# A hybrid attention trunk on one core: what follows a product moves one step ahead, two weight casts go ahead of two copies, and the last keys are loaded one phase earlier

## The chip, the core and the metric

The kernel runs on one core of one Trainium2 chip. The metric is the device time of one execution in microseconds (us), lower is better. TensorE (PE) multiplies, VectorE (DVE), ScalarE (ACT) and GpSimd (POOL) work elementwise, SyncE (SP) issues most of the transfers. Each engine works through its own queue in order; engines wait for each other through semaphores.

## The reference

One layer of a decoder trunk on x (2048 x 1024), all in float32. Cut to what matters here:

```python
mod = silu(c) @ w_ada + b_ada
shift, scale, gate = split(mod, 3)
u = x * (1 + scale) + shift
q, k, v, a_gate, p_in, p_gate, m_a, m_p = split(u @ w_in)
a = (sliding_window_sink_attention(q, k, v, sinks, bias, mask) * silu(a_gate)) @ w_attn_proj
p = (grouped(multiscale_causal_pool(p_in)) * pool_scale * silu(p_gate)) @ w_pool_proj
y = (sigmoid(m_a) * a + sigmoid(m_p) * p) @ w_out * (1 + gate)
x = layer_norm(alpha * x + y)
```

The attention has 16 query heads on 2 key heads of width 64. Each block of 128 queries looks at its own block of keys and the one before it, under a causal window of 128, with a relative bias for each head and one sink logit for each head. The pool is a causal mean over 2, 4, 8 or 16 steps, by channel group, less the input.

## The kernel before

**Products.** Every large product runs as a Strassen-like scheme on 2 x 2 blocks, with seven products in place of eight, named B11, T1, T2, B21, T3, B22, T4. A `Quad` holds two tiles of 128 output channels and the raw weights for them (`w`, four blocks of 128 x 512 named by `block`, and `a22`); `sum1`, `mid` and `late` make the sums of the weight blocks. To keep float32 accuracy each operand is split into a high part, rounded to the matmul's type by a cast, and a low part, the rest (`low`, line 131). One `product` (line 317) is therefore 12 matmuls of 128 x 128 by 128 x 512: four contraction tiles, and for each of them high x high, high x low and low x high. A quad has three accumulators in PSUM: a, b and c. B11 and B21 add into a, T1 and B22 into b, T2, T3 and T4 into c. Between the products there is elementwise work: c starts as a copy of a after B11 (`seed`), p5 is a copy of b after T1, b = c + p5 after T2, p5 = c + p5 after T3, and a result is handed on after B21 (a), B22 (b) and T4 (c and p5).

**Phases.** The sequence is cut into two halves of 1024 (s = 0 and 1). For each half there is a ring phase (`ring`, `back`, `front`), which does nothing but products (the gates, the keys and values, the first queries), and then an attention phase (`attention`, line 774). After both halves comes the phase of the projections and the output. `kv_quad` (line 543) is the quad of the keys and values in the ring. When its first result arrives, `place_kv` (line 1521) lays out the tiles `kk` (keys, a high and a low part) and `vv` (values), whose room had been lent to the ring as spare space until then; `take_k` (line 734) fills the keys, `turn_v` (line 720) transposes and fills the values some steps later. Column block 0 of `kk` and `vv` is the last block of the half before. `load_kv` (line 748) fetches it with two transfers from DRAM and does nothing for s = 0.

**The attention phase.** It runs 64 iterations, one for a pair of heads j and a block b of 128 queries (n = 8j + 4t + b), and three more for the end of the pipeline. In iteration n the code emits, in this order: the scores of n on TensorE (`score_mms`: rows `lg<-kk,qs`), the transposes of the probabilities of n-2 (`turn_mms`: rows `pt<-ident,L`), the reciprocal of the sums of n-1, the output of n-3 (`o`), the scaling of n-1, the high part `pth` of n-2, bias and exponential of n (`L`), the low part `ptl` of n-2, then the fill, then the product with the values of n-2 (`value_mms`: rows `pv<-pth,vv` and `pv<-ptl,vv`), and last the work whose time has come (`run_coming`). Every instruction there is emitted through `Ordered` (line 51), so each engine runs them in the order in which they are emitted. Line 57 stands in the profile for all of them.

**The fill.** `filling` (line 947) is a generator that goes through the 93 products of 13 quads (pool mix, merge gates, queries) and two opened ones. It gives out a product in four parts of three matmuls, and each iteration asks for five or six parts, so that 372 parts are spread over 67 iterations (line 1065). `begun(i)` runs before a product, among other things to split the weights of the product three places on (`split`, line 892: cast on ScalarE, low part on POOL or VectorE). `ended(i)` (line 927) emits what follows a product:

```python
if name == "T1":
    p5 = st[x][3] = tp.tile([P, CH], F32, tag="p5", bufs=2, name="p5")
    act.copy(p5, b)
elif name == "T2":
    dve.tensor_tensor(b, c, p5, ALU.add)
elif name == "T3":
    dve.tensor_tensor(p5, c, p5, ALU.add)
```

and for B21, B22 and T4 it calls `take`, which hands the result to the pool (`take_p`: three copies on ScalarE, sums on POOL), to the queries (`take_q`: two instructions on ScalarE and two on VectorE) or to a gate's store (`take_gate`: a copy and a transfer). Because `ended(i)` stands behind the `yield` of the last part, it runs when the next part is asked for, which is in the next iteration if the product ended with an iteration's last part.

**The start of the phase** (lines 985 to 996) emits, ahead of the loop: `load_kv`, the first bias tile, a one-element Exp that loads ScalarE's table (`warm`), the copy of a (`seed(0)`, row `mm<-mm`), the copy of b to p5 (row `p<-mm`), and then the splits of the first three products (T2, B21, T3 of quad 0; rows `w_set<-W`).

Of the kernel before, what the change touches and what calls it, by code (L numbers as in the profile page):

```python
# [60 lines left out]
def kernel(  # L61
# [66 lines left out]
    def as32(ap):  # L128
        return ap.bitcast(F32)

    def low(engine, dst, src, hi):
        engine.tensor_tensor(dst, src, as32(hi), ALU.subtract)  # L132

    def mm(*args, **kw):
        pe.matmul(*args, **kw)
# [6 lines left out]
    def bank(tag="mm"):  # L142
        return ps.tile([P, CH], F32, tag=tag, bufs={"mm": 4, "lg": 2, "pt": 1, "pv": 1}[tag], name=tag)
# [173 lines left out]
    def product(acc, w, name, first=False, i0=0, i1=4):  # L317
        t = sets[name]
        hi, lo = w
        for n, (part, u) in enumerate(((hi, 0), (hi, 1), (lo, 0))):  # L320
            for i in range(i0, i1):
                mm(
                    acc,
                    part[:, i * P : (i + 1) * P],
                    t[:, i, u, :],
                    start=first and i == 0 and n == 0,
                    stop=i == 3 and n == 2,
                    skip_group_check=True,
                )
# [213 lines left out]
    def kv_quad(s):  # L543
        vts = []

        def consume(ph, mi, t, src):
            if mi == 0:
                if t == 0:
                    place_kv(ph)
                take_k(ph, s, t, src)  # L550
            else:
                vt = ph.c("vt")
                nc.scalar.copy(vt, src)
                vts.append((t, vt))

        def turn(ph, i):
            turn_v(ph, s, *vts[i])

        return Quad((win[TK], win[TV]), consume), turn
# [160 lines left out]
    def turn_v(ph, s, t, vt):  # L720
        vtp = bank(("pt", "pv")[t]).rearrange("p (b a d) -> p b a d", b=NB, a=2)
        for b in range(NB):
            pe.transpose(vtp[:, b].rearrange("p a d -> p (a d)"), vt[:, b * P : (b + 1) * P], ident)
        blocks = slice(1 + NB * t, 1 + NB * (t + 1))
        for kv in range(2):
            dst = ph.c("v1", F32R).rearrange("p (b d) -> p b d", b=NB) if kv else vv[:, blocks]
            nc.scalar.copy(dst[:, :, 0:HD], vtp[:, :, kv, :])
            low(nc.vector, dst[:, :, HD:], vtp[:, :, kv, :], dst[:, :, 0:HD])
            if kv:
                sp.dma_start(v_d[s, :, blocks], as32(dst))  # L730
            elif s == 0 and t == 1:
                sp.dma_start(v_end_d, as32(dst[:, NB - 1]))

    def take_k(ph, s, t, kp):
        c0 = P + t * CH
        for kv in range(2):
            rows = slice(kv * HD, kv * HD + HD)
            dst = ph.t.tile([P, 2, CH], F32R, tag="k1", bufs=1, name="k1") if kv else kk[:, :, c0 : c0 + CH]
            for half in (kv, 1 - kv):
                to = slice(half * HD, half * HD + HD)  # L740
                nc.scalar.copy(dst[to, 0, :], kp[rows, :])
                low(nc.vector, dst[to, 1, :], kp[rows, :], dst[rows, 0, :])
            if kv:
                sp.dma_start(k_d[s, :, :, c0 : c0 + CH], as32(dst))
            elif s == 0 and t == 1:
                sp.dma_start(k_end_d, as32(dst[:, :, CH - P :]))

    def load_kv(s):
        if s:
            sp.dma_start(as32(kk[:, :, 0:P]), k_end_d)  # L750
            sp.dma_start(as32(vv[:, 0]), v_end_d)
# [22 lines left out]
    def attention(ph, s, fills, post, opened):  # L774
# [10 lines left out]
        def bias_tile(j):  # L785
            bt = tp.tile([P, 2, 2 * P], F32, tag="bt", bufs=2, name="bt")
            e_src = e_rep[:, 2 * j : 2 * j + 2, :]
            sp.dma_start(bt, bass.AP(e_src.tensor, e_src.offset + P - 1, [[HEADS * ET - 1, P], [ET, 2], [1, 2 * P]]))
            return bt
# [75 lines left out]
        def take(x, mi, t, src, kept=False):  # L865
            kind, m, _ = fills[x]
            if kind == "mix":
                take_p(m + mi, t, src)
            elif kind == "q":
                n = 8 * (m - 2 + mi) + NB * t + NB - 1  # L870
                if kept and n > now_n[0]:
                    later(n, lambda: take_q(m + mi, t, src, act, dve))
                else:
                    take_q(m + mi, t, src, act, dve)
            else:
                take_gate(kind, m + mi, t, src, kept)
# [5 lines left out]
        splits = {}  # L882
# [9 lines left out]
        def split(i):  # L892
            x, name = seq[i]
            q = quads[x]
            if name == "B11" and x > 1:
                q.sum1(pool)
            w = ph.split()
            hi, lo = made[i] = w[:, 0:CH], w[:, CH:]
            act.copy(hi, q.block(name))
            low(dve if name == "T1" or (x, name) in on_dve else pool, lo, q.block(name), hi)  # L900
            if name == "T1":
                q.mid(pool)
            elif name == "B21":
                q.late(pool)

        def begun(i):
            x, name = seq[i]
            if name == "T1":
                st[x][1] = bank()
                if x < K:  # L910
                    later(free_b[0], lambda: seed(x))
                    if free_b[0] < now_n[0]:
                        run_coming()
            if name == "B11":
                st[x] = [bank(), None, None, None]
                if x < K:
                    quads[x + 1].load(ph, False, sp, None)
            if (x, name) == (K - 1, "B22"):
                quads[K + 1].load(ph, False, sp, None)
            for j in splits.get(i, ()):  # L920
                split(j)

        def seed(x):
            st[x][2] = bank()
            act.copy(st[x][2], st[x][0])

        def ended(i):
            x, name = seq[i]
            if x >= K or name == "B11":
                return  # L930
            a, b, c, p5 = st[x]
# [7 lines that stand above are left out]
            elif name == "B21":  # L939
                take(x, 0, 0, a)  # L940
            elif name == "B22":
                take(x, 0, 1, b)
            else:
                take(x, 1, 0, c)
                take(x, 1, 1, p5, True)

        def filling():
            for i, (x, name) in enumerate(seq):
                begun(i)
                w = made.pop(i)  # L950
                acc = st[x][{"B11": 0, "B21": 0, "T1": 1, "B22": 1}.get(name, 2)]
                for k in range(4):
                    product(acc, w, name, name in ("B11", "T1"), k, k + 1)
                    yield
                ended(i)

        def score_mms(j, b, q, x):
            k0 = P if s == 0 and b == 0 else 0
# [25 lines left out]

        N = KT * 2 * NB
        U = 2 * NB
        load_kv(s)
        bts = {0: bias_tile(0)}
        act.activation(warm, mhalf, AF.Exp)
        seed(0)  # L990
        p5 = st[0][3] = tp.tile([P, CH], F32, tag="p5", bufs=2, name="p5")
        act.copy(p5, st[0][1])
        for i in range(-3, 0):
            for j in splits.get(i, ()):
                split(j)
        fill = filling()
        lgs, exps, Ls, pvs, outs, ags = {}, {}, {}, {}, {}, {}
        total, done = 4 * len(seq), 0

        for n in range(N + 3):  # L1000
            now_n[0] = n
            j, t, b = n // U, n // NB % 2, n % NB
# [511 lines left out]
    def rooms_of(name, dt=F32):  # L1514

        q = [kvp.tile([P, D], dt, tag=f"qs{i // 2}{i % 2}", name=f"{name}_qs{i}") for i in range(4)]
        k = kvp.tile([P, 2 * (P + 2 * CH)], F32, tag="kk", name=f"{name}_kk")
        v = kvp.tile([P, (2 * NB + 1) * P], F32, tag="vv", name=f"{name}_vv")
        return q, k, v

    def place_kv(ph):

        nonlocal kk, vv
        ph.turns.clear()
        kk = kvp.tile([P, 2, P + 2 * CH], F32R, tag="kk", name="kk")
        vv = kvp.tile([P, 2 * NB + 1, P], F32R, tag="vv", name="vv")
# [15 lines left out]
    with Pools("g0", spare=2, p=2, c=5) as ph:  # L1542
        started = head(ph, plans[0])
        kq, k, v = rooms_of("first", F32R)
# [7 lines left out]
    with Pools("g1", spare=4, p=2, c=5) as ph:  # L1552
        kq, k, v = rooms_of("second")
# [7 lines left out]
    with Pools("mix", spare=4, p=2, c=8) as ph:  # L1561
# [10 lines left out]
        for n, (raw, i) in enumerate((raw, i) for raw in (ain_d[1], pin_d[1], wo_d) for i in range(4)):  # L1572
            for offset, f in sums_to(ph, raw, i, load_raw(raw, i)):
                at = int(2 + 8 * n + offset)
                i, gi = every[at // 14]
# [78 lines left out]
```

## Time and profile before

| what | us |
|---|---|
| median of 3 runs | 1692.15 |
| lowest and highest run | 1687.09, 1692.64 |
| the profiled execution | 1693.3 |
| its span, first to last instruction | 1691.5 |
| first ring phase ends, first attention phase begins | about 256 |
| second ring phase ends, second attention phase begins | about 830 |
| projections begin | about 1183 |

The profile is of one execution. A span is the time from the first to the last instruction; the execution's own time is 1.8 us longer. Times in rows are us from the span's start. In a row of the timeline the last bracket is the engine's idle time just before, and what ended it. A matmul's duration runs from its start to a modelled end, and matmuls overlap.

### The profile page before, as it was taken

The numbers are of one execution on the slowest core, as the hardware profiler recorded it, in microseconds if no ns is written. First come the engines' busy times: TensorE is split into PE (matmuls) and PEld (weight loads), VectorE is DVE, ScalarE is ACT, GpSimd is POOL, SyncE is SP. The second block draws the span as 40 slices with busy tenths as digits, with TensorE's granted clock in tenths as the row PEclk, the third lists the DMA queues.
The fourth block names the chain that finished last, engine by engine and source line by source line (L and its number), as shares of the span: only waits on it lengthen the run. The fifth ranks groups of instructions, "written<-read, shape, count | busy, mean of one in ns | idle before, by whom it ended". The sixth has DMA issues, their size and how long they took to land.

```text
span 1691.5 us, 24675 instructions
## 1 busy us (share of the span) xinstructions
PE 1648.7 (97%) x8058; PEld 1384.4 (82%) x8058; DVE 1193.7 (71%) x2132; ACT 1030.0 (61%) x2150; POOL 988.5 (58%) x734
## 2 busy tenths in 40 slices
PE   7999999999999999999999999999999999999997
PEld 6788888888888888888788888888878777887886
DVE  6856545676857657357567677676669897989877
ACT  4755457878778755335578777876646445644452
POOL 3343437586857828762476867496567576533442
PEclk9999999999999999999999999999999999999999
DMA  9688843343432478766533344234979797888443
GB/s 359 219 279 307 197 161 102 101 132 108 149 107 99 135 248 308 267 231 211 190 114 99 114 130 156 81 114 135 336 247 363 262 360 259 318 283 271 150 150 112
DMA packets 188849, 336.79 MB, mean 199 GB/s; under 512 B 18336, under 2 KB 44080, under 8 KB 188720
## 3 DMA queue, kind: packets, MB, share of 16 engines
q1 hardware_dynamic: 185600, 330.96, 57.3%
q10 hardware_dynamic: 3088, 4.23, 1.0%
q8 instruction: 64, 1.05, 0.2%
q14 instruction: 65, 0.53, 0.1%
q0 software_dynamic: 32, 0.02, 0.0%
HBM read 227.96 MB, written 110.33 MB: 200 GB/s over the span
## 4 chain that ended last, share of the span: by engine, by line
PE 74%; DVE 8%; DMA 7%; ACT 4%; issue 3%; POOL 3%; SPq 1%; POOLq 0%; DVEq 0%; ACTq 0%
PE mm L57 48%; PE lg L57 19%; PE pv L57 4%; PE pt L57 4%; DVE w_set L132 1%; DMA ain_T<-spare 1%; ACT L L57 1%; DMA g<-ma_d 1%; DMA g<-mp_d 1%; DVE w_set L57 1%; DVE set_T L57 1%; POOL W L269 1%; DMA spare<-pin_B 1%; DVE L L57 1%; ACT w_set L57 1%
## 5 line engine op out<-in xcount | busy, mean ns | idle before, releaser
L57 PE MATMUL mm<-set_B,w_set 128*128 128x512 f32 x2664 | 655.8, 393 | 2.2 <-DVE w_set L132 1.2
L57 PEld LDWEIGHTS mm<-set_B,w_set 128*128 128x128 f32 x2664 | 497.1, 189 | 107.0 <-DVE w_set L132 2.4
L57 PE MATMUL mm<-set_T,w_set 128*128 128x512 f32 x1824 | 455.5, 396 | 5.9 <-DVE mm L57 3.9
L57 PE MATMUL lg<-set_T,w_set 128*128 128x512 f32 x1704 | 412.6, 392 | 10.5 <-DVE p L390 4.4
L57 PEld LDWEIGHTS mm<-set_T,w_set 128*128 128x128 f32 x1824 | 336.7, 189 | 76.2 <-DVE mm L57 6.5
L57 PEld LDWEIGHTS lg<-set_T,w_set 128*128 128x128 f32 x1704 | 319.9, 189 | 81.8 <-ACT w_set L306 5.2
L132 DVE TENSOR_TENSOR w_set<-W,w_set 128x1024 fp32r<-128x1024 f32 x137 | 197.8, 1445 | 142.3 <-ACT w_set L306 129.3
L306 ACT CAST w_set<-W 128x1024 fp32r<-128x1024 f32 x137 | 143.8, 1050 | 212.7 <-PE mm L57 124.3
L57 POOL TENSOR_TENSOR w_set<-W,w_set 128x512 fp32r<-128x512 f32 x120 | 157.3, 1318 | 116.9 <-ACT w_set L57 112.0
L269 POOL TENSOR_TENSOR W<-W,A 128x512 f32<-128x512 f32 x46 | 74.1, 1610 | 232.5 <-DMA A<-in_win_dram 63.5
L57 DVE TENSOR_TENSOR o<-pv,o 64x128 f32<-64x128 f32 x256 | 72.1, 282 | 133.7 <-ACT o L57 127.3
L57 POOL TENSOR_TENSOR spare<-spare 128x512 f32<-128x512 f32 x68 | 124.0, 1826 | 31.5 <-DMA spare<-pin_B 12.2
L57 POOL TENSOR_TENSOR W<-W 128x512 f32<-128x512 f32 x82 | 108.3, 1336 | 53.2 <-DVE sm L57 31.0
L57 ACT ACTIVATE L<-L,nm 128x257 f32<-128x257 f32 (+1 forms) x256 | 127.2, 499 | 9.3 <-DVE nm L57 3.7
L278 POOL TENSOR_TENSOR W<-W 128x512 f32<-128x512 f32 x46 | 72.8, 1583 | 95.9 <-DVE w_set L132 83.5
L57 DVE CUSTOM_DVE_ANT_0 L<-lg,bt,nsink 128x256 f32<-128x256 f32 (+1 forms) x256 | 111.7, 473 | 21.3 <-PE lg L57 11.9
L57 ACT CAST w_set<-W 128x512 fp32r<-128x512 f32 (+1 forms) x165 | 101.4, 628 | 20.9 <-POOL W L57 14.9
L273 POOL TENSOR_TENSOR W<-W 128x512 f32<-128x512 f32 x44 | 72.7, 1656 | 66.3 <-DVE w_set L132 57.2
L57 ACT COPY o<-pv 64x256 f32<-64x256 f32 x128 | 47.4, 370 | 75.9 <-PE pv L57 74.7
L57 DVE TENSOR_TENSOR ptl<-pt,pth 128x512 fp32r<-128x512 f32 (+1 forms) x128 | 85.7, 669 | 1.3 <-ACT pth L57 1.0
L274 POOL TENSOR_TENSOR W<-W 128x512 f32<-128x512 f32 x44 | 71.6, 1628 | 21.9 <-DMA W<-in_win_dram 18.9
L57 ACT ACTIVATE L<-L,sm 128x256 f32<-128x256 f32 (+1 forms) x128 | 64.3, 502 | 31.7 <-DVE sm L57 31.4
(230 smaller groups left out, 2398.2 us busy)
## 6 DMA issues: line engine op xcount, KB each, us to landing
W<-in_win_dram SPq DMA_DIRECT2D x42, 512.0 KB, 5.4
W<-in_win_dram SPq DMA_DIRECT2D x42, 256.0 KB, 3.7
A<-in_win_dram SPq DMA_DIRECT2D x42, 256.0 KB, 4.9
ag_d<-sig SPq DMA_DIRECT2D x32, 256.0 KB, 5.7
pg_d<-sig SPq DMA_DIRECT2D x32, 256.0 KB, 4.4
pg<-pg_d SPq DMA_DIRECT2D x32, 256.0 KB, 3.2
pin_B<-fin SPq DMA_DIRECT2D x32, 256.0 KB, 2.0
ag<-ag_d SPq DMA_DIRECT2D x32, 256.0 KB, 2.9
```

What stands on the lines that cost most here:

```text
L57: return lambda *args, **kw: self.tc.keep_in_program_order(op(*args, **kw))
L132: engine.tensor_tensor(dst, src, as32(hi), ALU.subtract)
L269: e.tensor_tensor(self.w[:, 1, :], self.w[:, 2, :], self.a22, ALU.add)
L273: e.tensor_tensor(x[:, 1, :], x[:, 1, :], x[:, 0, :], ALU.subtract)
L274: e.tensor_tensor(x[:, 2, :], x[:, 0, :], x[:, 2, :], ALU.subtract)
L278: e.tensor_tensor(x[:, 3, :], x[:, 3, :], x[:, 1, :], ALU.subtract)
L306: a.copy(by_two(hi), raw)
```

## The change

Three edits. `load_kv(s)` moves from the start of the attention phase to the moment in the ring where `place_kv` has just laid out the tiles. `ended(i)` is called behind the last part's matmuls and ahead of their `yield`, in place of behind it. At the start of the attention phase the splits of the first two products and `seed(0)` come first, then the one-element Exp, then the copy to p5, then the split of the third product.

```diff
@@ kv_quad
             if mi == 0:
                 if t == 0:
                     place_kv(ph)
+                    load_kv(s)
                 take_k(ph, s, t, src)
@@ filling
                 for k in range(4):
                     product(acc, w, name, name in ("B11", "T1"), k, k + 1)
+                    if k == 3:
+                        ended(i)
                     yield
-                ended(i)
@@ attention
-        load_kv(s)
         bts = {0: bias_tile(0)}
+        for i in (-3, -2):
+            for j in splits.get(i, ()):
+                split(j)
+        seed(0)
         act.activation(warm, mhalf, AF.Exp)
-        seed(0)
         p5 = st[0][3] = tp.tile([P, CH], F32, tag="p5", bufs=2, name="p5")
         act.copy(p5, st[0][1])
-        for i in range(-3, 0):
-            for j in splits.get(i, ()):
-                split(j)
+        for j in splits.get(-1, ()):
+            split(j)
```

## The prediction, made before the changed kernel ran

> **What bounds the kernel now.** First the page: the busy times and the chain that ended last.
>
> ```profile
> PE 1648.7 (97%) x8058; PEld 1384.4 (82%) x8058; DVE 1193.7 (71%) x2132; ACT 1030.0 (61%) x2150; POOL 988.5 (58%) x734
> ...
> PE 74%; DVE 8%; DMA 7%; ACT 4%; issue 3%; POOL 3%; SPq 1%; POOLq 0%; DVEq 0%; ACTq 0%
> ```
>
> TensorE sets the time. The change takes no matmul away, so it can only shorten the moments in which TensorE stands still. It touches the two attention phases and one load in the ring ahead of the second, so I cut the windows view at the two phases:
>
> ```profile
> 256.00:620.00 364.00, 358.71 (x1919) 307.16 (x1918) 245.63 (x675) 272.14 (x735) 254.19 (x207) 1.00 0.38 124
> ...
> 830.00:1183.00 353.00, 349.30 (x1899) 300.58 (x1900) 243.17 (x667) 267.89 (x725) 252.32 (x199) 1.00 0.37 118
> ```
>
> The first numbers are start and length, then the busy times of PE, PEld, DVE, ACT and POOL. TensorE lacks 5.3 us of the first phase and 3.7 us of the second, so the prize is a few us. The longest row of TensorE's waits in the first phase's window and that in the second's (us, times, longest) show one place:
>
> ```profile
> PE mm L57 <- DVE mm L57: 2.4, 2, 1.6
> ...
> PE mm L57 <- DVE mm L57: 1.5, 2, 1.0
> ```
>
> For a yardstick, an iteration of the attention loop without waits, from the chain in order of time (start, us):
>
> ```profile
> 1150.91 0.47 PE pv L57 x4
> 1151.39 0.47 PE lg L57 x4
> 1151.85 0.44 PE pt L57 x4
> 1152.29 4.12 PE mm L57 x18
> ```
>
> 18 product matmuls take 4.12, so 0.23 each. The page's rows give one a duration of 0.39, because they overlap: a wait costs 0.16 more than the idle time shown.
>
> **Part 1: casts ahead of copies.** The start of the first phase, from the timeline (start, us, engine, what, idle before in brackets):
>
> ```profile
> 249.77 1.48 POOL L273 TENSOR_TENSOR W<-W 128x512 f32<-128x512 f32 x1
> 253.69 0.57 ACT L57 COPY mm<-mm 128x512 f32<-128x512 f32 x1 [2.00 <-PE mm L57]
> 256.16 0.56 PE L57 MATMUL lg<-kk,qs 128*128 128x128 f32 x4
> 256.36 0.59 ACT L57 COPY p<-mm 128x512 f32<-128x512 f32 x1 [2.10 <-PE mm L57]
> 256.84 1.66 ACT L57 CAST w_set<-W 128x512 fp32r<-128x512 f32 x3
> 257.51 0.73 PE L57 MATMUL mm<-set_T,w_set 128*128 128x512 f32 x2 [0.80 <-ACT w_set L57]
> 257.54 2.52 POOL L57 TENSOR_TENSOR w_set<-W,w_set 128x512 fp32r<-128x512 f32 x2 [6.29 <-ACT w_set L57]
> 258.87 3.97 PE L57 MATMUL mm<-set_T,w_set 128*128 128x512 f32 x10 [0.62 <-POOL w_set L57]
> 264.26 0.64 PE L57 MATMUL lg<-kk,qs 128*128 128x256 f32 x4
> ```
>
> ScalarE is in order. The cast of the first fill product (T2) stands behind the copy `p<-mm`, which waits for the T1 product to end at 256.16. Yet T2's raw weights are there at 251.25, when POOL's L273 ends. TensorE then waits for the high part, and again for POOL's low part. Iteration 0 should take 0.47 + 4.12 = 4.59 (it has no `pt` and no `pv`). It takes 264.26 - 256.16 = 8.10, so 3.51 too long.
>
> After the change two casts (1.66/3 = 0.55 each) run on ScalarE after 251.25, in the idle time ahead of 253.69. POOL makes two lows (2.52) from about 251.9 to 254.4; its row shows it idle there for 6.29. Both are done before T1 ends at 256.16, with 1.7 us to spare. The copy at 253.69 is released by TensorE and at most 0.1 later. The third cast stays behind `p<-mm`; it serves T3, two products (5.5 us) later. The Exp warm-up goes behind the copy at 253.69, where ScalarE has 2.10 idle. I count the whole 3.51, in two pieces. Waiting explains 1.80: 0.80 + 0.62, and 0.16 twice, come to 1.74. The rest, 1.71, is a slower clock:
>
> ```profile
> 256.30:259.71 3.41, 1.99 (x11) 1.26 (x10) 0.63 (x4) 3.34 (x6) 2.17 (x2) 1.00 0.30 111
> 259.71:263.12 3.41, 3.41 (x10) 2.65 (x9) 0.17 (x1) 1.93 (x7) 3.33 (x4) 0.50 0.00 0
> 447.44:450.86 3.42, 1.97 (x11) 1.72 (x12) 2.05 (x4) 2.06 (x6) 3.42 (x4) 1.00 0.68 221
> ```
>
> The last three numbers are granted clock, DMA share and GB/s. After a window with TensorE busy for 1.99, it ran 3.41 us at clock 0.50, which costs 3.41 x 0.5 = 1.71. The third row shows as little busy time without a drop behind it, so the stall does not always bring one. Bounds 0 and 1.71; I take 1.71, since the wait and the drop stand next to each other.
>
> The Trainium skill, "TensorE: Matmul & The Clock Gate", section "Why this matters for your kernels", puts the fall to half clock at one whole window of idle, gaps of more than about 3 us. By that rule the 1.80 of waiting would not have caused this drop, it could come again anywhere, and the sum would be 1.71 smaller; this trace disagrees where it dropped after a window that was over half busy.
>
> **Part 2: the last keys loaded in the ring.** The second phase's start, timeline and, for `kk`, landing time:
>
> ```profile
> 826.81 2.88 PE L57 MATMUL mm<-set_T,w_set 128*128 128x512 f32 x12
> 827.49 0.53 SPq L57 DMA_DIRECT2D kk<-k_end_d  x1
> 830.36 0.71 PE L57 MATMUL lg<-kk,qs 128*128 128x256 f32 x4 [0.67 <-ACT p L57]
> 836.06 0.64 PE L57 MATMUL lg<-kk,qs 128*128 128x256 f32 x4
> ...
> DMA to landing us min/median/max: 2.7/2.7/2.7
> ```
>
> T1 (12 matmuls, 2.75) ends at 829.56, and the scores start 0.80 later. The wait is put down to ScalarE's copy, which the scores do not need; the transfer of the last keys, issued at 827.49 and landing 2.7 later (830.19), is what they need. Iteration 0 then takes 5.70 instead of 4.59: 1.11 of the same wait for weights as in the first phase, without a drop of the clock. So this start gives 0.80 + 1.11 = 1.91.
>
> The two loads move to the kv quad's first result on SP's queue:
>
> ```profile
> L741 ACT CAST kk<-mm x4: 576/579/581, 763.4 to 778.5; 64x512 fp32r<-64x512 f32 x4
> ...
> L57 SPq DMA_DIRECT2D pin_T<-second_kk x4: 337/380/401, 705.2 to 713.0; - x4
> ...
> 750.61 1.92 SPq L57 DMA_DIRECT2D spare<-in_wout_dram  x4
> 764.77 0.33 SPq L262 DMA_DIRECT2D W<-in_win_dram  x1
> ```
>
> The first row is the first write to `kk`, the second the last store out of its room, the others SP's queue (start, us). The room was last read by that store, issued at 713.0, so the load waits for nothing. SP stands idle from 752.53 to 764.77, and the two issues (0.53 each by the row above) fit in between. Cost 0; if SP were full there, 1.1 us on the next weight load. In the first phase the function does nothing.
>
> **Part 3: what follows a product is given out with its last matmuls.** A product is four parts of three matmuls, and an iteration hands out five or six parts (372 parts in 67 iterations). What follows used to be emitted when the next part is asked for. That makes a difference only where a product ends with an iteration's last part. Counting `-(-372*(n+1)//67)`, that is so 17 times a phase, 13 of them with something to follow: T3 at n=1, T1 at 4, 9, 14, 19, B22 at 17, 22, 27, 32, T2 at 35, 40, 45, 50. After T2, VectorE adds c to p5, and T3, which writes c again, must wait for that. At n=35:
>
> ```profile
> 442.98 0.40 PE L57 MATMUL pv<-pth,vv 128*128 128x256 f32 x2
> 446.90 1.33 DVE L57 TENSOR_SCALAR L<-L,sm 128x256 f32<-128x256 f32 x1
> 448.15 0.69 DVE L57 TENSOR_TENSOR mm<-mm,p 128x512 f32<-128x512 f32 x1
> 448.89 1.65 PE L57 MATMUL mm<-set_T,w_set 128*128 128x512 f32 x6 [1.56 <-DVE mm L57]
> ```
>
> T2 ended ahead of 442.98; the add came at 448.15, behind iteration 36's softmax. Moved, it runs by about 444 and T3 starts with no wait for it. The two rows `PE mm <- DVE mm` above are these waits: 2.4 + 1.5 = 3.9 in four, plus 4 x 0.16: 4.5. At n=40 and 45 the add is just in time today, gain 0.
>
> What may be late instead: the moved ScalarE and VectorE instructions now wait for the last matmul with the next iteration's softmax queued behind them, and the `pv` matmuls wait for that. A row of such an order exists already, where take_q is emitted at the end of an iteration (n=31); beside it an iteration with slack (n=28):
>
> ```profile
> 403.58 0.69 DVE L57 TENSOR_TENSOR ptl<-pt,pth 128x512 fp32r<-128x512 f32 x1
> 406.57 0.40 PE L57 MATMUL pv<-pth,vv 128*128 128x256 f32 x2
> ...
> 423.45 2.87 DVE L57 SCALAR_TENSOR_TENSOR qs<-p,qs 64x512 fp32r<-64x512 f32 x2
> 427.70 0.50 PE L57 MATMUL pv<-pth,vv 128*128 128x256 f32 x2 [0.45 <-ACT pth L57]
> 428.43 0.50 PE L57 MATMUL pv<-ptl,vv 128*128 128x256 f32 x2 [0.23 <-DVE ptl L57]
> ```
>
> There the wait was 0.45 + 0.23 + 0.32 = 1.0. Of the moved ones, T1's copy (0.59) goes where ScalarE waits for `pv` anyway; B22 at 17, 27 and 32 brings more than one instruction. At n=28 `ptl` ends 2.3 us ahead of its use and take_q holds VectorE back by about 1.5, so it should be free. Bounds 0 and 6 x 1.0 = 6; I take 0.5. SP's store behind the gate copy (n=22) and POOL's sums behind B22 come one iteration earlier, with no new wait.
>
> **Sum.** 3.51 + 1.91 + 4.5 - 0.5 = 9.4 us. The profiled execution took 1693.3 (span 1691.5, 1.8 around it); less 9.4 is 1683.9. The median of the three runs, 1692.15, is 1.15 lower. I forecast 1683.
>
> **Rivals.**
> (a) The weights or POOL's lows bind T3 as soon as the add is early, so part 3 gives nothing: 1683 + 4.5 = 1687.5. For it: POOL is busy 3.42 of 3.42 in the window at 447.44. Against: the low part that follows T3's is due only 2.7 us on. Chance 0.12.
> (b) The casts get no earlier, because something orders them behind T1 anyway: part 1 fails, 3.51 + 1.11 lost: 1687.6. Against: the raw weights are there at 251.25. Chance 0.06.
> (c) The wait goes and the drop of the clock stays: the row at 447.44 shows that the two are not tied, so the 3.41 us at 0.50 may fall on another place of the span: 1683 + 1.71 = 1684.7. Chance 0.12. The rule of the Trainium skill's page "TensorE: Matmul & The Clock Gate" leads there.
> (d) Slower: head-of-line blocking. If each of the 26 moved places costs the 1.0 of n=32, that is 26 - 9.9 = 16 more than the median: 1708. It decides from 0.6 a place ((9.9 + 5)/26). Against: the slack of 2.3. Chance 0.05.
>
> **Numbers.** The forecast itself has 0.65. A measurement tells about 0.3% (5.1 us) from no change, so (a) and (b), 4.6 us faster, fall just within it: of their 0.18 I give 0.06 to faster and 0.12 to same. The forecast and (c) together hold 0.77; 0.73 of that to faster, 0.03 to same, 0.01 to slower. (d) is slower. Faster 0.79, same 0.15, slower 0.06. Range: above, the bound of the new waits, 6 instead of 0.5, gives 1688.5, and (a) and (b) lie under that: 1689. Below, no new wait gives 1682.5, and as the three runs of before spread over 5.5 us (1687.09 to 1692.64), I go 5 further: 1677.5.
>
> **What would show it.** Iteration 0 of both phases near 4.6 us; no granted clock of 0.50 near 260; no wait of `lg` at the second phase's first scores; no row `PE mm <- DVE mm` in either phase. Wrong: new `pv <- pth` or `ptl` waits at n=18, 28, 33, or ScalarE casts still after 256.

## The result, and the profile after

| | median us | lowest to highest | runs |
|---|---|---|---|
| before | 1691.05 | 1685.97 to 1692.64 | 8 |
| after | 1695.53 | 1694.38 to 1698.78 | 8 |

The ratio is 1.0033, with a 95% interval of 1.0018 to 1.0047. The forecast was 1683, with a range up to 1689. The sign is wrong: by the medians the changed kernel is 4.5 us slower.

The page of the profiled execution after (1698.78, span 1697.0):

```profile
PE 1650.6 (97%) x8058; PEld 1387.0 (82%) x8058; DVE 1199.2 (71%) x2132; ACT 1026.7 (61%) x2146; POOL 988.0 (58%) x734
...
PE 66%; DVE 10%; POOL 9%; ACT 6%; DMA 4%; issue 4%; SPq 0%; POOLq 0%; DVEq 0%; ACTq 0%
```

The busy times are those of before. In the chain, POOL has gone from 3% to 9% and TensorE from 74% to 66%, so something behind POOL has taken a place on the path. The windows over the two phases (the columns are those shown of before):

```profile
257.00:621.00 364.00, 358.04 (x1908) 306.52 (x1907) 242.53 (x673) 269.40 (x733) 251.25 (x205) 0.99 0.37 122
833.00:1186.00 353.00, 347.61 (x1885) 299.02 (x1884) 240.77 (x665) 266.06 (x723) 248.45 (x196) 1.00 0.36 115
```

TensorE now lacks 6.0 and 5.4 us, against 5.3 and 3.7. TensorE's longest rows of waits for other engines (us, times, longest) in the first phase, and then in the second:

```profile
PE pv L57 <- ACT pth L57: 3.6, 3, 2.2
PE pv L57 <- DVE ptl L57: 1.4, 4, 0.6
PE mm L57 <- ACT mm L57: 0.8, 1, 0.8
```

```profile
PE mm L57 <- ACT mm L57: 2.0, 1, 2.0
PE pv L57 <- DVE ptl L57: 1.9, 5, 0.6
PE pv L57 <- ACT pth L57: 1.4, 1, 1.4
```

The rows `PE mm <- DVE mm` are gone, as predicted. What replaces them waits for the softmax (`pth`, `ptl`) and for ScalarE's seed copy (`mm`).

Where in the phases this happens comes from the start times of the rows `lg<-kk,qs`: the length of each iteration less the yardstick. That is 5.49 for an iteration with six parts, as most show (the prediction's four rows add up to 5.50), and 0.23 less for each of three matmuls with five parts, so 4.81. It is 0.91 less at n = 0 and 1, which have no `pt` and `pv`. Where a block of the first phase has no keys ahead of it, an iteration comes out some 0.45 shorter; that is not counted. The lost time of one profiled execution of each kernel, in us, phase 1 / phase 2:

| place | before | after |
|---|---|---|
| start (n=0; in phase 2 with the wait of the first scores) | 3.52 / 1.92 | 0 / 0 |
| T2 (n=36, 51, 59, 60) | 4.56 / 3.04 | 3.87 / 1.25 |
| n=32 | 1.13 / 1.27 | 0.45 / 0.57 |
| n=8, 16 | 0 / 0.23 | 1.00 / 1.09 |
| n=22, 23, 38, 40 | 0 / 0 | 6.47 / 6.73 |

The first three lines fall from 15.4 to 6.1, which is 9.3 and close to the 9.4 of the forecast. The last two rise from 0.2 to 15.3. The differences sum to +5.8; the spans differ by 1697.0 - 1691.5 = 5.5, so the rest of the program nearly cancels. The first scores start 1.7 later (256.16 and 257.85), which isn't the change's doing as far as is known: in the traces of all kernels here they start between 256.05 and 259.92. About 1.5 comes back after the attention phases.

**What happens at n=22.** The timeline after, of the moment behind iteration 21 (first phase):

```profile
371.81 1.03 POOL L57 TENSOR_TENSOR nxt<-vb 128x514 f32<-128x514 f32 x1
372.92 1.04 POOL L57 TENSOR_TENSOR fin<-nxt 128x512 f32<-128x512 f32 x1
374.00 1.75 DVE L57 SCALAR_TENSOR_TENSOR fin<-fin,p 128x512 f32<-128x512 f32 x1 [4.54 <-POOL fin L57]
375.67 0.15 DVE L57 RECIPROCAL sm<-sm 128x2 f32<-128x2 f32 x1
375.86 0.51 ACT L57 ACTIVATE L<-L,sm 128x256 f32<-128x256 f32 x1 [4.97 <-DVE sm L57]
376.39 0.59 ACT L57 CAST pth<-pt 128x512 fp32r<-128x512 f32 x1
377.03 0.80 PE L57 MATMUL pv<-pth,vv 128*128 128x256 f32 x2 [2.21 <-ACT pth L57]
```

Read it from the bottom. TensorE waits 2.21 for the high part `pth`, whose cast stands behind ScalarE's scaling, which waits 4.97 for VectorE's reciprocal. The reciprocal stands behind `fin<-fin,p`, the pool's `second` step, which has held VectorE still for 4.54 us because POOL's sums for it end only at 373.96, and which then takes 1.75. `take_p` (line 833) counts its slot from the iteration in which it is *emitted*: `n = max(now_n[0], pool_free[1] + 1, pool_free[0] + 3)`. With B22's follow-up emitted one iteration sooner, the four slots of the quad with window 4 go from 16, 18, 19, 21 to 16, 17, 19, 20, and those of window 8 from 31, 33, 34, 36 to 31, 32, 34, 35. So `second` of the fourth result is now emitted at the end of n=21 and n=37, one iteration earlier, to the head of VectorE's queue, with the whole softmax of the next iteration behind it. The same result before:

```profile
374.92 1.04 POOL L57 TENSOR_TENSOR fin<-nxt 128x512 f32<-128x512 f32 x1
...
375.46 0.40 PE L57 MATMUL pv<-pth,vv 128*128 128x256 f32 x2
...
376.43 0.68 DVE L57 SCALAR_TENSOR_TENSOR fin<-fin,p 128x512 f32<-128x512 f32 x1
```

POOL's sums end even later there, at 375.96, but VectorE comes to `second` one iteration later, and neither it nor TensorE waits.

**What happens at n=40** in the second phase, timeline after:

```profile
1038.78 0.56 ACT L57 COPY raw<-mm 128x512 f32<-128x512 f32 x1
...
1040.02 1.29 POOL L57 TENSOR_TENSOR fin<-fin,pg 128x512 f32<-128x512 f32 x1
...
1041.34 0.33 SPq L57 DMA_DIRECT2D pin_B<-fin  x1
...
1041.76 0.38 SPq L57 DMA_DIRECT2D ma_d<-raw  x1
...
1046.99 0.59 ACT L57 COPY raw<-mm 128x512 f32<-128x512 f32 x1 [3.88 <-DMA ma_d<-raw]
...
1047.47 0.59 ACT L57 COPY mm<-mm 128x512 f32<-128x512 f32 x1
...
1048.12 1.19 PE L57 MATMUL mm<-set_T,w_set 128*128 128x512 f32 x4 [2.00 <-ACT mm L57]
```

The gate copy `raw` is ready at 1039.34, but its store leaves SP at 1041.76, behind the store `pin_B<-fin`, which waits for POOL. The place of that store is counted from `take_p`'s slot too. Before, it came an iteration later, and the gate's store left straight behind its copy (1032.37 to 1032.94):

```profile
1032.96 0.33 SPq L57 DMA_DIRECT2D ma_d<-raw  x1
...
1040.10 0.33 SPq L57 DMA_DIRECT2D pin_B<-fin  x1
```

`raw` has one buffer (line 862). The next copy into it waits until the store has landed, with the seed copy `mm<-mm` behind it on ScalarE, and T2's matmuls wait for that.

**The clock.** Windows with the granted clock third from the end, each pair the stall and what followed (after):

```profile
373.54:376.95 3.41, 1.28 (x6) 0.74 (x4) 2.90 (x7) 1.07 (x3) 2.78 (x3) 1.00 0.17 63
376.95:380.36 3.41, 3.26 (x13) 2.97 (x14) 3.21 (x10) 3.08 (x10) 1.00 (x2) 0.50 0.29 111
...
1045.96:1049.38 3.42, 1.42 (x7) 1.06 (x7) 0.34 (x2) 2.36 (x5) 1.16 (x2) 1.00 0.53 201
1049.38:1052.79 3.41, 3.41 (x11) 2.73 (x10) 2.14 (x8) 2.79 (x9) 0.98 (x2) 0.50 0.39 124
```

Both new stalls are followed by 3.4 us at half clock, so the one at n=40 costs 3.86 and not 2.00.

### The profile page after: what moved, and what is told of

The parts are those of the page before. It is cut to its first block, busy times and chain, and to the rows that moved or that the text cites. A ratio compares the mean times of both kernels' runs of the same rounds, so it can differ in the third digit from the quotient of the medians.

```text
span 1697.0 us, 24679 instructions
## 1 busy us (share of the span) xinstructions
PE 1650.6 (97%) x8058; PEld 1387.0 (82%) x8058; DVE 1199.2 (71%) x2132; ACT 1026.7 (61%) x2146; POOL 988.0 (58%) x734
## 4 chain that ended last, share of the span: by engine, by line
PE 66%; DVE 10%; POOL 9%; ACT 6%; DMA 4%; issue 4%; SPq 0%; POOLq 0%; DVEq 0%; ACTq 0%
PE mm L57 41%; PE lg L57 19%; PE pv L57 3%; PE pt L57 3%; POOL fin L57 2%; POOL w_set L57 2%; POOL W L57 2%; POOL nxt L57 2%; DVE w_set L132 1%; DVE set_T L57 1%; ACT L L57 1%; ACT w_set L57 1%; DVE L L57 1%; DVE wide L630 1%; DVE w_set L57 1%
## 5 line engine op out<-in xcount | busy, mean ns | idle before, releaser
L132 DVE TENSOR_TENSOR w_set<-W,w_set 128x1024 fp32r<-128x1024 f32 x137 | 201.7, 1472 | 139.7 <-ACT w_set L306 127.0
L57 PE MATMUL lg<-kk,qs 128*128 128x256 f32 (+1 forms) x512 | 81.0, 280 | 0.0
```

The lines of the kernel that those rows point to most:

```text
L57: return lambda *args, **kw: self.tc.keep_in_program_order(op(*args, **kw))
```

## The experiments

The theory, after the traces: the loss is in B22's follow-up, through `take_p`'s earlier slots and POOL's lateness, and it comes at few places. The main rival is the one of the prediction: waits at all moved places, T1's and T3's too. Each ratio is to the before of the same chip and has its 95% interval; runs 8 and 10 are one execution each and have none. Losses are in us, first phase / second phase, worked out as in the table above.

**1. Nothing handed out early** (parts 1 and 2 alone).

```diff
-                    if k == 3:
-                        ended(i)
                     yield
+                ended(i)
```

> The changed kernel with part 3 taken back (what follows a product comes behind the last part's yield again); parts 1 and 2 stay. Theory P (the earlier B22 results move the pool's slots in take_p, and VectorE's pool instruction then waits for POOL ahead of the softmax) and theory Q (any instruction moved to the head of the queues holds the softmax back) both expect the gain of the two starts and no new wait: 3.5 + 1.9 = 5.4 us under the kernel before, 1685.7 by its 1691.05. Theory S (the starts themselves cost what they gain, by shifting the phases) expects 1691 or more.

Measured 1686.82 against 1692.18: 0.9971 (0.9961 to 0.9982), which is 4.9 us. Parts 1 and 2 do bring their share (the forecast had 5.4 for them); the loss of the whole is in part 3.

**2. All early but B22.**

```diff
-                    if k == 3:
+                    if k == 3 and name != "B22":
                         ended(i)
                     yield
+                if name == "B22":
+                    ended(i)
```

> The changed kernel, but what follows B22 stays behind the yield; T1, T2 and T3 are early. Theory P: the long waits at n=22, 38 and 40 are gone and the four waits of T3 on VectorE stay gone: 5.4 + 4.5 = 9.9 under the kernel before, about 1681; with the 0.7 of n=16 in each phase 1682.5. Theory Q: T1's copies and the adds hold the softmax back as well, so it stays above 1688.

Measured 1685.43: 0.9966 (0.9952 to 0.9979). n=22, 38 and 40 lose nothing; n=16 still loses 0.69 / 0.76. The time is 3 us above the 1682.5 of theory P: n=59 and 60 of the first phase lose 3.84, where run 1 has 1.51.

**3. All early, the pool's slots as before.** The slot is counted one iteration on when the follow-up comes with an iteration's last part.

```diff
-            n = max(now_n[0], pool_free[1] + 1, pool_free[0] + 3)
+            n = max(now_n[0] + last_part[0], pool_free[1] + 1, pool_free[0] + 3)
...
+                last_part[0] = int(done + 1 == -(-total * (n + 1) // (N + 3)))
                 next(fill)
```

> The changed kernel as it is, but take_p counts its slot from the next iteration when a product ended with an iteration's last part, so the pool's work has its old slots while gate copies and queries stay early. Theory P: about 1682, as with B22 late. Theory Q: about 1695, since nothing is taken off the heads of the queues but the pool's copies.

Measured 1685.47: 0.9965 (0.9952 to 0.9977). With every follow-up early and only the pool's slots held back, n=22, 23, 38 and 40 lose nothing in either phase, though the time is 3 us above the expected 1682, as in run 2. So it is the slot, and not the early emission of B22's first instructions.

**4. Only B22 early, on the kernel before.**

```diff
+                    if k == 3 and name == "B22":
+                        ended(i)
                     yield
-                ended(i)
+                if name != "B22":
+                    ended(i)
```

> The kernel before with only what follows B22 moved ahead of the yield; no other part of the change. Theory P: the waits at n=22, 38 and 40 appear alone, 3.4 + 0.9 + 2.3 at n=22 and some 6 at n=38 and 40 in the two phases: 10 to 14 slower than before, 1701 to 1705. Theory Q: a part of that, 4 of the 13 moved places, about 1695.

Measured 1700.31: 1.0053 (1.0041 to 1.0065). This part alone costs 9 us by the ratio, just under the 10 to 14 expected. n=22 and 23 lose 4.48 / 3.67, n=40 0.87 / 3.84; of the places of after, only n=38 loses nothing.

**5. Only T2 early** (beside parts 1 and 2).

```diff
-                    if k == 3:
+                    if k == 3 and name == "T2":
                         ended(i)
                     yield
+                if name != "T2":
+                    ended(i)
```

> The changed kernel with only T2's sum early; T1's copy, T3's sum and B22's results stay behind the yield. If T1's early copy at n=14 is what brings POOL's work onto VectorE's query instructions (n=16: 0.69 and 0.76 too long in the two phases with T1, T2 and T3 early), these two go, and n=59 of the first phase stays too long, since POOL is what it waits for: 1.4 under the kernel with the three early, about 1684. If n=16 comes from elsewhere, 1685.4 as there.

Measured 1685.36 against 1691.08: 0.9959 (0.9945 to 0.9974). Against run 1 that is about 2 us better in the ratio, where the forecast gave T2 4.5, but the intervals overlap. The trace shows n=36 and 51 without loss in both phases, and n=59 and 60 of the first phase at 2.25 + 1.80 where run 1 has 1.24 + 0.28: 2.5 of 3.1 us come back there. n=16 loses nothing.

**6. The pool's second step one iteration later**, for windows under 8.

```diff
-            wait = 1 if POOL_W[m // 2] < 8 else 2
+            wait = 2
```

> The changed kernel, but take_p gives VectorE's instruction (which waits for POOL's sums) out two iterations after its slot for the windows 2 and 4 as well, instead of one; ScalarE's copies and POOL's sums stay early. If n=22 is VectorE waiting for POOL at the head of its queue, the 3.35 + 0.9 and 2.27 there go, and n=38 and 40 (window 8, two already) stay: about 6 less than the changed kernel, 1690. If ScalarE's earlier copies are the cause, it stays at 1695 or more.

Measured 1690.18 against 1691.08: 0.9999 (0.9986 to 1.0013). By the ratios that is 5.7 us under after, where 6 were expected. The trace shows n=22 without loss; n=38, whose `wait` was 2 already, keeps 1.09 / 0.81. n=40 was expected to stay and falls from 1.02 / 3.86 to 0.70 / 0.45 (see run 7). The timeline at n=22:

```profile
373.24 1.04 POOL L57 TENSOR_TENSOR fin<-nxt 128x512 f32<-128x512 f32 x1
...
374.95 0.40 PE L57 MATMUL pv<-pth,vv 128*128 128x256 f32 x2
...
376.06 1.78 DVE L57 SCALAR_TENSOR_TENSOR fin<-fin,p 128x512 f32<-128x512 f32 x1
```

POOL's sums end at 374.28, no earlier than after (373.96), but VectorE takes them when the softmax is through, and `pv` waits for nothing. That confirms the head of VectorE's queue, and not POOL's own work, as the cause at n=22. The profiled execution (1687.2) is 3 us under the median of the 12 runs (1684.16 to 1696.22); which wait the longer ones have isn't known.

**7. The gate's store issued by ScalarE**, right behind its own copy, in place of SP.

```diff
-            later(now_n[0], lambda: sp.dma_start(gates_d[name][s, m, t], x))
+            later(now_n[0], lambda: (sp if kept else act).dma_start(gates_d[name][s, m, t], x))
```

> The changed kernel with the store of the gate's copy (raw) issued from ScalarE's queue and not from SP's, where it stood behind a store that waits for POOL. If the wait of the first T2 matmuls at n=40 (1.0 and 3.9 too long) comes from that store's late issue and the one buffer of raw, it goes: about 4.9 less than the changed kernel, 1690.6, less what ScalarE pays for the issues. If not, n=40 stays as it is.

Measured 1693.12 against 1691.08: 1.0013 (1.0002 to 1.0025). By the ratios that is some 3 us under after, where 4.9 were expected, but the intervals overlap. In the second phase n=40 goes from 3.86 to 0, as the timeline shows:

```profile
1036.64 0.57 ACT L57 COPY raw<-mm 128x512 f32<-128x512 f32 x1
1037.24 0.33 ACTq L57 DMA_DIRECT2D ma_d<-raw  x1
...
1041.51 0.59 ACT L57 COPY raw<-mm 128x512 f32<-128x512 f32 x1 [0.54 <-DMA ma_d<-raw]
```

The store leaves 0.03 behind the copy, and the next copy waits 0.54 in place of 3.88. In the first phase n=40 still loses 1.38. The chain of waits there, in order of time (start, us):

```profile
462.35 6.16 DMA ma_d<-raw
...
468.59 0.59 ACT raw L57
...
469.57 0.58 ACT mm L57
```

Here the way from issue to release takes 6.16. So in the second phase the loss goes when the store leaves SP's queue; in the first, one buffer and a slow store are enough. The late place on SP's queue isn't enough by itself either, as run 6 shows at n=40 of its second phase:

```profile
1033.65 0.38 SPq L57 DMA_DIRECT2D ma_d<-raw  x1
...
1036.94 0.59 ACT L57 COPY raw<-mm 128x512 f32<-128x512 f32 x1 [1.95 <-PE lg L57]
```

There the store leaves behind `pin_B<-fin` as after, but the buffer is free at most 3.3 us later, not 5.2, and the copy waits for no transfer. Why the same store is slow in one kernel and not in the other isn't known; the last weight load on SP was issued 1.9 us before the store in after and 2.9 before it in run 6. n=22 and 23 lose 4.7 / 2.2, much as after.

**8. Only the last keys loaded in the ring, on the kernel before** (one execution).

```diff
                     place_kv(ph)
+                    load_kv(s)
...
-        load_kv(s)
```

> The kernel before with the last keys and values loaded in the ring and nothing else. The first scores of the second phase start with the end of T1, 0.8 earlier in it than before, and iteration 0 stays 1.1 too long, since the casts are late as before; no new wait on SP's queue in the ring. If the scores waited for the copy that the row names, they still start 0.8 late.

Measured 1690.64 in one run. The scores of the second phase no longer wait, but iteration 0 then loses 1.95 and not 1.12, where the 1.1 of before was expected: a miss. Its timeline:

```profile
826.31 2.88 PE L57 MATMUL mm<-set_T,w_set 128*128 128x512 f32 x12
829.03 0.63 PE L57 MATMUL lg<-kk,qs 128*128 128x256 f32 x4
...
830.44 0.73 PE L57 MATMUL mm<-set_T,w_set 128*128 128x512 f32 x2 [0.78 <-ACT w_set L57]
...
831.80 1.42 PE L57 MATMUL mm<-set_T,w_set 128*128 128x512 f32 x5 [0.63 <-POOL w_set L57]
```

The 0.80 saved ahead of the scores is spent a moment later waiting for the weights. By this trace part 2 alone buys nothing.

**9. Only the casts ahead, on the kernel before.**

```diff
         bts = {0: bias_tile(0)}
-        act.activation(warm, mhalf, AF.Exp)
+        for i in (-3, -2):
+            for j in splits.get(i, ()):
+                split(j)
         seed(0)
+        act.activation(warm, mhalf, AF.Exp)
...
-        for i in range(-3, 0):
-            for j in splits.get(i, ()):
-                split(j)
+        for j in splits.get(-1, ()):
+            split(j)
```

> The kernel before with the casts ahead of the copies and nothing else. Iteration 0 of the first phase takes 4.6, that of the second too, behind scores that still start 0.8 late: 3.5 (or 1.8, where no drop of the clock was there to lose) and 1.1 under the kernel before, about 1688.

Measured 1688.20 against 1692.23: 0.9978 (0.9964 to 0.9992). Phase 1 starts without loss. Iteration 0 of phase 2 loses 1.70, where no loss was expected: a miss. All of the 1.70 is 3.4 us at half clock from 829.7 on. The wait for the keys stands just ahead of it, and it is longer than the 0.8 expected:

```profile
828.63 0.71 PE L57 MATMUL lg<-kk,qs 128*128 128x256 f32 x4 [2.36 <-DMA kk<-k_end_d]
```

**10. Only T1 early** (beside parts 1 and 2, one execution).

```diff
-                    if k == 3:
+                    if k == 3 and name == "T1":
                         ended(i)
                     yield
+                if name != "T1":
+                    ended(i)
```

> The changed kernel with only T1's copies early. If they bring POOL's sums onto VectorE's query instructions, n=16 is 0.7 too long in both phases and n=8 some 0.1 more than before, with the waits of T3 on VectorE at n=36 and 51 as in the kernel before. If it was T3 or the sums, n=16 is as in the kernel before.

Measured 1686.26 in one run. n=16 loses 0.69 / 0.75, all that T1 adds; the 0.1 expected at n=8 is not there. The timeline of this kernel, and of run 5 (T1 late) at the same point:

```profile
337.58 1.28 POOL L57 TENSOR_TENSOR W<-W,A 128x512 f32<-128x512 f32 x1
337.68 3.42 DVE L57 SCALAR_TENSOR_TENSOR qs<-p,qs 64x512 fp32r<-64x512 f32 x2 [0.49 <-ACT qs L57]
```

```profile
338.06 2.53 DVE L57 SCALAR_TENSOR_TENSOR qs<-p,qs 64x512 fp32r<-64x512 f32 x2 [0.42 <-ACT qs L57]
338.30 1.75 POOL L57 TENSOR_TENSOR W<-W,A 128x512 f32<-128x512 f32 x1
```

VectorE's two instructions take 3.42 against 2.53 when POOL's sum of weights starts just ahead of them. T1's copy comes at 332.36 and not at 335.89, so the next cast on ScalarE starts at 335.64 and not at 336.36 (run 5's trace runs 0.4 later as a whole). POOL's low part follows that cast, and so POOL's sum starts 0.1 ahead of VectorE's two instructions and not 0.2 behind their start.

**11. T2 and B22 early, T1 and T3 late, the pool's slots as before.** This is run 3's edit and, in `filling`:

```diff
-                    if k == 3:
+                    if k == 3 and name not in ("T1", "T3"):
                         ended(i)
                     yield
+                if name in ("T1", "T3"):
+                    ended(i)
```

> The changed kernel with T2's sum and B22's results early, the pool's slots counted as before the change, T1's copy and T3's sum behind the yield. If T1's copies are what costs 0.7 at n=16 and 0.3 at n=8, and the early query result at n=27 is what shortens n=32 by some 0.7, this is the best of the set: about 1 under the kernel with T2 alone early, 1684, with no wait at n=16, 22, 38 and 40. If not, n=16 is still 0.7 too long.

Measured 1681.68 (1679.25 to 1684.29) against 1692.23: 0.9940 (0.9921 to 0.9959). This beats both kernels. TensorE's waits in its first phase:

```profile
PE pv L57 <- ACT pth L57: 1.1, 1, 1.1
PE pv L57 <- DVE ptl L57: 0.8, 2, 0.6
```

n=16, 22, 38 and 40 lose nothing; n=32 loses 0.43 / 0.57. Against run 3 the lost time in the traces falls by 3.3 us, but the intervals of the two overlap.

## Why the prediction was wrong

**The step that failed** is the last sentence of part 3: "SP's store behind the gate copy (n=22) and POOL's sums behind B22 come one iteration earlier, with no new wait." They do come earlier, but so does VectorE's `second`, because `take_p` counts from `now_n`. Run 4, with B22's follow-up alone early, is 9 us slower than before. Run 3 takes only the slot back, and the ratio goes from 1.0033 to 0.9965, some 11 us. Run 6 delays only `second` for the windows under 8, and the loss at n=22 goes. The sentence names POOL and SP, and not the VectorE instruction that waits for POOL; nor does it ask when POOL would be through, although the prediction's own row at 447.44 shows POOL busy for a whole window. With the slot taken back, run 3 gains 5.9 us and not 9.4; the difference is in the terms for T2 and T1 below.

**Part 1** (3.51 + 1.11) holds: iteration 0 takes 4.54 and 4.58 after. These are rows of the timeline of the first phase's start, after:

```profile
257.85 0.56 PE L57 MATMUL lg<-kk,qs 128*128 128x128 f32 x4
258.05 0.59 ACT L57 COPY p<-mm 128x512 f32<-128x512 f32 x1 [0.64 <-PE mm L57]
...
258.24 2.95 PE L57 MATMUL mm<-set_T,w_set 128*128 128x512 f32 x12
```

T2 starts right behind the scores with no wait. But the 1.71 of half clock is not in every execution with late casts: iteration 0 of the first phase lost 1.91 in run 4 and 1.89 in run 8, without a drop.

**Part 2** (0.80) holds only together with part 1, as run 8 shows. Together they bring 0.29% in run 1, which is 4.9 us of 1692.18, against the 5.4 of the sum. How long the scores wait for the keys differs too: 0.80 before, 2.4 in run 9.

**T2** (4.5) was mis-sized. The waits at n=36 and 51 go in both phases, but n=59 and 60 of the first phase lose 2.3 more, a stretch of half clock included; over both phases the four places gain 2.5 in the traces. VectorE's `second` waits for POOL there, 4.61 after and 3.54 before, so POOL looks like the bound; no run tested that.

**T1**: "T1's copy (0.59) goes where ScalarE waits for `pv` anyway". The copy itself costs nothing (the iterations behind 4, 9, 14 and 19 show no loss), but n=16 loses 0.7 in each phase, because a cast and POOL's work behind the copy come earlier (run 10). The 0.3 at n=8 is there with T1 and T3 early (run 2) and not with T1 alone.

**The new waits** were bounded by 0 and 6, taken as 0.5, and measure 13.2 + 1.9 in the traces (half clock included), less the 1.4 that n=32 gains. The size was wrong because the row at n=32, taken as dearest, has its input ready within an iteration; a queue's head that waits for another busy engine had no row before.

**The rivals.** (a) and (b) are out: the `mm <- DVE mm` waits are gone, n=36 and 51 lose nothing, and the casts come early. (c) is right that half clock turns up elsewhere: inside the attention phases, before had it at 259.7, after at 377.0, 574.9 and 1049.4; two of these stand right behind the new stalls. (d) had the right mechanism and the wrong places: n=18, 28 and 33, named in the prediction, lose nothing. Four places a phase lose 0.6 to 4.3 each instead of 26 losing 1.0. The price lies in who else is late, and less in the number of places.

## What to carry to other kernels

When an instruction is emitted earlier on an in-order engine, list every index that is counted from the moment of emission, and work out for each moved *consumer* when its producer will be through, not only whether the instruction itself has time. A consumer that heads its queue ahead of its producer stalls everything behind it, and a stall of some 2 us can cost nearly twice its length, since half clock can follow it (1.71 us here). Split such a change by kind, because the kinds differ in sign: here T1's part cost 1.4 in its trace, B22's lost 9 us until its slot was held back, and T2's and B22's parts with the slot held back came out best (0.9940).

## What was not expected of the hardware

**Half clock behind short stalls.** Clock 0.50 followed windows of 3.4 us in which TensorE was still busy for 1.28 (373.54) and 1.42 us (1045.96), where single stalls were 2.2 and 2.0 us; before, it followed 1.99 (256.30) but not 1.97 (447.44). So the busy share does not decide it alone. The Trainium skill, "TensorE: Matmul & The Clock Gate", section "Why this matters for your kernels", asks for a whole idle window, gaps of more than about 3 us; these rows disagree.

**VectorE beside POOL.** In run 9's trace of the first phase, by tile:

```profile
L57 DVE SCALAR_TENSOR_TENSOR qs<-p,qs x6: 685/1120/1690, 337.1 to 516.3; 64x512 fp32r<-64x512 f32 x6
...
L57 DVE SCALAR_TENSOR_TENSOR qs<-mm,qs x18: 683/688/694, 315.7 to 514.9; 64x512 fp32r<-64x512 f32 x18
```

The columns are minimum, median and maximum in ns. `qs<-p,qs` reads both inputs from SBUF and takes up to 1690; `qs<-mm,qs` reads one from PSUM and is never over 694. The Trainium skill, "SBUF — State Buffer", section "Who interferes with whom", says that a VectorE instruction with two inputs in SBUF contends with a GpSimd instruction that reads SBUF. The rows agree, and in runs 10 and 5 it makes 0.9 whether POOL's sum starts 0.1 ahead of VectorE's pair or 0.2 behind its start. No run tried the pair by itself.

**A short store can hold a buffer for long.** `ma_d<-raw` held its buffer for 5.2 us after, from its issue at 1041.76 to the copy at 1046.99, and for 6.16 in run 7's first phase, but for 3.3 at most in run 6. The forecast had taken it as free.
